# RWKV state as a full 128x128 block, and its diagonal blocks loaded by three transfers instead of one

## The chip, the cores and the metric

One core of a Trainium2 chip runs the whole program. The metric is the time of one execution in microseconds of the device. The engines named here are PE (TensorE: PE for the matmuls, PEld for the loads of their weights), DVE (VectorE), ACT (ScalarE), POOL (GpSimd, which also issues most small DMAs) and SP (SyncE, which issues the loads of the big weights).

## The reference, cut to what matters

Two blocks follow each other on 272 tokens (16 meta tokens and 256 real ones) of width 2048. The first block projects its normed input with `w_in` and runs three mixers side by side, HGRN2 (a), mLSTM (b) and RWKV7 (c), whose outputs are gated, projected and added. The second block has two layers with pooling, a state-space mixer and sparse attention. The change touches the RWKV7 mixer alone.

RWKV7 has 16 heads of width 64, and each has a state S of 64x64. In chunk form, with the decays folded into the operands, and with A, B, K, R and V of one head and one chunk of tokens, the kernel computes:

```
L   = strict lower part of  A B^T                  (per head: tokens x tokens)
u   = (I - L)^-1 ( A S + strict(A K^T) V )
y   = R S + incl(R B^T) u + incl(R K^T) V
S'  = decay * ( S + B^T u + K^T V )
```

The meta tokens (16) are the first chunk, with S = 0; two chunks of 128 real tokens follow.

## The kernel before

**Tiling.** All activations lie with features on the 128 partitions and tokens in the free dimension. One RWKV group is four heads on two partition tiles j = 0, 1: in each tile head hh = 0 owns partitions 0 to 63 and hh = 1 owns 64 to 127. There are four groups, and each has a `front_c` (projections and operands) and a `back_c` (the chunks).

**The projections and their order.** `unit` (L302) streams the weights: a chunk `wraw` of 128x1024 is loaded through SP, ACT copies it to `whi`, DVE forms the rest `wlo`, and PE runs 24 matmuls of 256 to 272 columns into a tile `pj`. `whi` and `wlo` have four buffers each. The mixers' `back_*` generators run beside these projections: every `yield` gives the turn to another stream, and the framework's planner (a simulated timeline) then fixes each engine's order of instructions at build time. On the chip each engine works that order off strictly: what stands behind a waiting instruction waits too. The projections' ACT and DVE steps have raised priority. PSUM tiles named `mx` (`pst`, L433) have four buffers, which all the small matmuls share.

**The diagonal blocks.** `base_start` (L654) gathers the 16x16 diagonal blocks of L for both chunks and the meta tokens (12 blocks on each partition) in `Dc`, writes them to a DRAM tile `ld`, and reads them back through POOL's queue with each row spread to 16 partitions, into `LB` of 15 steps x 12 x 16 (L666). `base_solve` (L669) then inverts these blocks by 15 steps of forward substitution; step j reads only `LB[:, j]`, one DVE product (`yt<-LB,yc`) and one DVE sum (`yc<-yc,yt`). Everything later in the `back_c` of that group needs its result. `LB` has one buffer, and each group fills it once.

**The chunks.** `back_c` (L947) makes the state S of 128 partitions x 2 x 64 after the meta tokens (L971 to L978): eight matmuls that each write one head's 64 partitions, then `ts` with the decay. For each of the two chunks it does the following. `inverse` completes the inverse Y from the blocks. The step that I call **ru** (L987 to L995) computes A S + strict(A K^T) V: for each head a matmul on the 64 rows of that head (`mx<-S,AT`), then one on 128 token rows (`mx<-vT,Lk`), 8 in all. L996 to L1002 multiply by Y (`mx<-ru,Y`). `pair` makes the two masked score matrices. The step that I call **py** (L1007 to L1013) computes y: for each head one matmul of 64 rows by 64 columns of weights (`mx<-RT,S`), then two of 128 rows by 64 columns (`mx<-Rb,u` and `mx<-Rk,vT`), 12 in all, every one into the 64 partitions of its head. After the first chunk the step **pz** (L1015 to L1025) brings S forward with eight matmuls of 64 weight columns and 64 moving columns.

A matmul on f32 operands appears in the trace as two MATMUL instructions (passes). A form such as 64*128 says rows x columns of the weights in the array, and the shape behind it is that of the moving operand.

Of the kernel before, what the change touches and what calls it, by code (L numbers as in the profile page):

```python
# [9 lines left out]
F32 = mybir.dt.float32  # L10
# [3 lines left out]
ALU = mybir.AluOpType  # L14
# [3 lines left out]
P = 128  # L18
NM = 16
# [219 lines left out]
class Kernel:  # L239
    def __init__(self, ctx, tc, ins, out, dbg=None, stop=None):  # L240
        self.ctx, self.tc, self.nc = ctx, tc, tc.nc
        self.ins, self.out, self.dbgs, self.stop = ins, out, dbg or {}, stop
        self.V, self.S, self.G, self.PE = tc.nc.vector, tc.nc.scalar, tc.nc.gpsimd, tc.nc.tensor

# [21 lines left out]
    def act(self, out, in_, func=AF.Copy, **kw):  # L266
        return self.S.activation(out, in_, func, **kw)  # L267

# [154 lines left out]
    def reg(self, *shape, rows=P, name="r"):  # L423

        n = math.prod(shape)
        t = self.rf.tile([P, 544], F32, tag="r", name=name, bufs=self.nrf)[:rows, :n]
        if len(shape) == 2:
            t = t.rearrange("p (a b) -> p a b", a=shape[0])
        elif len(shape) == 3:
            t = t.rearrange("p (a b c) -> p a b c", a=shape[0], b=shape[1])  # L430
        return t
# [222 lines left out]
    def base_start(self, Lb):  # L654

        Dc = self.Dc
        for c in range(2):
            t = self.reg(4, 8, 16, name="db")
            blk = self.cst("blk").unsqueeze(1).unsqueeze(3).to_broadcast([P, 4, 8, 16])
            self.tt(t, Lb[c].rearrange("p h (b u) -> p h b u", u=16), blk, ALU.mult, self.G)  # L660
            for w in (4, 2):
                self.tt(t[:, :, :w], t[:, :, :w], t[:, :, w:2 * w], ALU.add, self.G)
            self.tt(Dc[:, 4 * c:4 * c + 4], t[:, :, 0], t[:, :, 1], ALU.add, self.G)
        ld = self.dr.tile([8, 16 * 192], F32, tag="ld", name="ld", bufs=2)
        self.nc.gpsimd.dma_start(ld.rearrange("b (s f) -> (b s) f", s=16), Dc.rearrange("p a b -> p (a b)"))
        self.nc.gpsimd.dma_start(self.LB.rearrange("p s a b -> p (s a b)"),  # L666
                                 ld[:, :15 * 192].unsqueeze(1).to_broadcast([8, 16, 15 * 192]))

    def base_solve(self):  # L669

        y = self.reg(12, 16, name="yc")
        self.G.tensor_copy(y, self.cst("eye16").unsqueeze(1).to_broadcast([P, 12, 16]))
        tmp = [self.early(12, 16, name="yt") for _ in range(2)]
        for j in range(15):
            t = tmp[j % 2][:, :, j + 1:]
            self.mul(t, self.LB[:, j, :, j + 1:], y[:, :, j:j + 1].to_broadcast([P, 12, 15 - j]))
            self.add(y[:, :, j + 1:], y[:, :, j + 1:], t)
            yield 0.3
        return y
# [110 lines left out]
    def start_c(self):  # L790
        p1 = self.p1
        self.hw0 = p1.tile([P, 16], F32, name="hw0")
        self.ts(self.hw0, self.par("w0", 0, 16), 0.5, ALU.mult)
        self.wup = p1.tile([P, 1024], F32, name="wup")
        self.nc.gpsimd.dma_start(self.wup, self.ins["wup"])
        self.yc = [None] * 4
        self.Dc = p1.tile([P, 12, 16], F32, name="Dc")
        self.G.memset(self.Dc, 0.0)
        self.LB = p1.tile([P, 15, 12, 16], F32, name="LB")

    def front_c(self, g):
        p1, reg = self.p1, self.reg
# [144 lines left out]
    def back_c(self, g, ops):  # L947
        gl, AT, BT, KT, RT, Lm, Lb, bk, bkm, bon, vT, vm, z = ops
        p1, reg = self.p1, self.reg
        f0 = 2 * g  # L950
        fl = lambda t: t.rearrange("p a b -> p (a b)")
        sm = lambda *shape, name, rows=P, bufs=1: p1.tile([rows, *shape], F32, tag="s_" + name, name=name, bufs=bufs)
        heads = [(j, hh, slice(64 * hh, 64 * hh + 64)) for hh in range(2) for j in range(2)]

        pu = self.pst()
        pu3 = pu[:NM, :256].rearrange("p (h v) -> p h v", h=4)
        for i, (j, hh, rr) in enumerate(heads):
            self.mm(pu3[:, i], Lm[:, i], vm[:, j, rr])
        ru = reg(4, 64, rows=NM, name="rum")
        self.act(ru, pu3)  # L960
        base = yield from self.base_solve()
        Ym = base[:NM, 8:]
        yield 1.0
        pu = self.pst()
        pu3 = pu[:NM, :256].rearrange("p (h v) -> p h v", h=4)
        for i in range(4):
            self.mm(pu3[:, i], Ym[:, i], ru[:, i])
        um = reg(4, 64, rows=NM, name="um")
        self.act(um, pu3)
        yield 1.0  # L970
        S = sm(2, 64, name="S", bufs=3)  # L971
        pz_ = self.pst()
        pz3 = pz_[:, :P].rearrange("p (j v) -> p j v", j=2)
        for i, (j, hh, rr) in enumerate(heads):
            self.mm(pz3[rr, j], bkm[:, 0, j, rr], um[:, i], start=True, stop=False)
            self.mm(pz3[rr, j], bkm[:, 1, j, rr], vm[:, j, rr], start=False, stop=True)
        for j in range(2):
            self.ts(S[:, j], pz3[:, j], gl[:, j, 0:1], ALU.mult)  # L978
        yield 1.0

        y = reg(2, NR, name="y")
        for c in range(2):
            strict, incl = self.cst("si")[:, :P], self.cst("incl")
            Y = yield from self.inverse(Lb[c], base[:, 4 * c:4 * c + 4])
            Lk = self.pair(KT, AT, c, strict, "Lk")
            yield 1.0
            ru = reg(4, 64, name="ru")  # L987
            for hh in range(2):
                pu = self.pst()
                pu3 = pu[:, :P].rearrange("p (h v) -> p h v", h=2)  # L990
                rr = slice(64 * hh, 64 * hh + 64)
                for j in range(2):
                    self.mm(pu3[:, j], AT[rr, 2 * j + c], S[rr, j], start=True, stop=False)
                    self.mm(pu3[:, j], Lk[:, 2 * hh + j], vT[:, 2 * j + c, rr], start=False, stop=True)
                self.act(ru[:, 2 * hh:2 * hh + 2], pu3)  # L995
            yield 1.0  # L996
            pu = self.pst()
            pu3 = pu[:, :256].rearrange("p (h v) -> p h v", h=4)
            for i in range(4):
                self.mm(pu3[:, i], Y[:, i], ru[:, i])  # L1000
            u = reg(4, 64, name="u")
            self.act(u, pu3)  # L1002
            yield 1.0
            Rb = self.pair(BT, RT, c, incl, "Rb")
            Rk = self.pair(KT, RT, c, incl, "Rk")
            yield 1.0
            py = self.pst()  # L1007
            py3 = py[:, :256].rearrange("p (j t) -> p j t", j=2)
            for i, (j, hh, rr) in enumerate(heads):
                self.mm(py3[rr, j], S[rr, j], RT[rr, 2 * j + c], start=True, stop=False)  # L1010
                self.mm(py3[rr, j], u[:, i], Rb[:, i], start=False, stop=False)
                self.mm(py3[rr, j], vT[:, 2 * j + c, rr], Rk[:, i], start=False, stop=True)
            self.act(y[:, :, P * c:P * c + P], py3)  # L1013
            yield 1.0
            if c == 0:  # L1015
                pz_ = self.pst()
                pz3 = pz_[:, :P].rearrange("p (j v) -> p j v", j=2)
                for i, (j, hh, rr) in enumerate(heads):
                    self.mm(pz3[rr, j], bk[:, 0, j, rr], u[:, i], start=True, stop=False)
                    self.mm(pz3[rr, j], bk[:, 1, j, rr], vT[:, 2 * j, rr], start=False, stop=True)  # L1020
                S2 = sm(2, 64, name="S", bufs=3)
                self.add(S2, pz3, S)
                for j in range(2):
                    self.ts(S2[:, j], S2[:, j], gl[:, j, 1:2], ALU.mult)
                S = S2  # L1025
                yield 1.0

        pm = self.pst()
        self.mm(pm, self.cst("bd64"), fl(y))
        self.stt(y, pm.rearrange("p (j t) -> p j t", j=2), -1.0 / 64, ALU.mult, y, ALU.add)  # L1030
        yield 2.0
        sq = reg(2, NR, name="sq")
        self.act(sq, y, AF.Square)
        pm = self.pst()
        self.mm(pm, self.cst("bd64"), fl(sq))
        self.rstd(fl(sq), pm, 1.0 / 64, self.eps(1))
        yield 2.0
        for j in range(2):
            self.stt(y[:, j], y[:, j], self.par("ln_g", f0 + j), ALU.mult, sq[:, j], ALU.mult)
            self.stt(y[:, j], y[:, j], self.par("ln_b", f0 + j), ALU.add, bon[:, j], ALU.add)  # L1040
        self.stt(y, y, 0.5, ALU.mult, z, ALU.mult)
        self.dbg(f"c_o{g}", y)
        self.yc[g] = y
# [894 lines left out]
```

## Time and profile before

| | |
|---|---|
| median of 3 runs | 2994.66 us (2994.41 to 2998.49) |
| the profiled execution's own time | 2993.82 us |
| its span | 2992.0 us |
| PE busy | 2932.0 us, 98% of the span, 23566 matmul instructions |
| DVE busy | 2001.8 us, 67% |
| ACT busy | 1429.5 us, 48% |
| POOL busy | 162.3 us, 5% |
| loads of `LB` | 4, 1440.0 KB each |

A busy engine is not the same as a bound one: matmuls overlap in their pipeline, so what counts on PE is the distance from the start of one to the start of the next, and which waits end late. The RWKV work lies in the first third of the span: the first `yt<-LB,yc` starts at 100.4 us and the last matmul with S as weights or moving operand at 878.2 us.

### The profile page before, as it was taken

What the parts mean: (1) busy time and instruction counts of PE and PEld (TensorE: products, weight loads), DVE (VectorE), ACT (ScalarE), POOL (GpSimd) and SP (SyncE); (2) the same over time, 40 slices, a digit from 0 to 9 for tenths busy, and PEclk for the clock granted to TensorE, in tenths of its full rate; (3) what the DMA queues carried; (4) which work ended last, traced back from release to release, by engine and by line L of the source; (5) the groups of instructions that cost most, each with busy time, mean ns of one, the idle gap of its engine ahead of it and who ended that gap; (6) DMA issues with size and microseconds to landing.
All of it is one profiled execution on the core that took longest, in us unless ns stands there. A gap on an engine that the chain in (4) does not pass through costs nothing.

```text
span 2992.0 us, 57144 instructions
## 1 busy us (share of the span) xinstructions
PE 2932.0 (98%) x23566; PEld 2813.2 (94%) x23566; DVE 2001.8 (67%) x3512; ACT 1429.5 (48%) x2043; POOL 162.3 (5%) x317
## 2 busy tenths in 40 slices
PE   8899999999999999999999999999989999999997
PEld 8898999988889999999999899999989999999997
DVE  7657757746645555567976778774568777877555
ACT  6445645435444434456444444444555444544453
POOL 1000001001000000001100000000011000000000
PEclk9999999999999999999999999999999999999999
DMA  6533534524435666566555455555545645555553
GB/s 221 148 113 121 148 100 127 148 86 140 136 105 164 186 187 184 185 199 221 175 168 154 133 162 163 162 187 173 174 157 172 186 142 155 178 179 185 173 187 122
DMA packets 134005, 479.37 MB, mean 160 GB/s; under 512 B 17552, under 2 KB 18064, under 8 KB 133232
## 3 DMA queue, kind: packets, MB, share of 16 engines
q1 hardware_dynamic: 122112, 441.80, 47.7%
q0 software_dynamic: 11200, 32.84, 4.0%
q8 instruction: 184, 3.01, 0.4%
q10 hardware_dynamic: 432, 1.09, 0.1%
q14 instruction: 77, 0.63, 0.1%
HBM read 467.35 MB, written 7.02 MB: 159 GB/s over the span
## 4 chain that ended last, share of the span: by engine, by line
PE 72%; issue 1%; DVE 1%; DMA 1%; ACT 0%; POOL 0%; DVEq 0%; ACTq 0%; POOLq 0%
PE pj L291 64%; PE mx L291 6%; PE mx L295 1%; DMA LB<-ld 1%; DVE out L270 0%; DVE h L270 0%; DVE xl L288 0%; DMA ed<-csd 0%; ACT L267 0%; DMA csd<-cs 0%; DVE wlo L270 0%; ACT whi L267 0%; ACT r L267 0%; DVE mix L288 0%; POOL ed L1816 0%
## 5 line engine op out<-in xcount | busy, mean ns | idle before, releaser
L291 PE MATMUL pj<-xh,whi 128*128 128x272 f32 (+2 forms) x6080 | 1752.4, 289 | 17.6 <-ACT xh L267 14.3
L291 PE MATMUL pj<-xh,wlo 128*128 128x272 f32 (+2 forms) x6080 | 1749.8, 288 | 15.3 <-DVE wlo L270 15.3
L291 PE MATMUL pj<-xl,whi 128*128 128x272 f32 (+2 forms) x6080 | 1746.3, 287 | 1.0 <-DVE xl L288 1.0
L267 ACT ACTIVATE whi<-wraw 128x1024 fp32r<-128x1024 f32 x840 | 887.0, 1058 | 1245.3 <-PE pj L291 1053.5
L270 DVE TENSOR_TENSOR wlo<-wraw,whi 128x1024 fp32r<-128x1024 f32 x840 | 1024.4, 1221 | 558.9 <-ACT whi L267 555.9
L291 PEld LDWEIGHTS pj<-xh,whi 128*128 128x128 f32 x6080 | 1145.5, 189 | 35.2 <-ACT xh L267 14.7
L291 PEld LDWEIGHTS pj<-xh,wlo 128*128 128x128 f32 x6080 | 1150.2, 189 | 27.4 <-DVE wlo L270 16.0
L291 PEld LDWEIGHTS pj<-xl,whi 128*128 128x128 f32 x6080 | 1148.3, 189 | 10.1 <-issue 4.8
L291 PE MATMUL pj<-yl,whi 128*128 128x256 f32 x384 | 108.2, 282 | 0.0
L291 PE MATMUL pj<-yh,wlo 128*128 128x256 f32 x384 | 108.0, 281 | 0.0
L291 PE MATMUL pj<-yh,whi 128*128 128x256 f32 x384 | 107.8, 281 | 0.0
L267 ACT ACT_TABLE_LOAD x79 | 101.4, 1283 | 3.1 <-PEq L1927 1.7
L291 PEld LDWEIGHTS pj<-yh,wlo 128*128 128x128 f32 x384 | 72.4, 189 | 0.0
L291 PEld LDWEIGHTS pj<-yh,whi 128*128 128x128 f32 x384 | 72.4, 189 | 0.0
L291 PEld LDWEIGHTS pj<-yl,whi 128*128 128x128 f32 x384 | 72.2, 188 | 0.0
L291 PE MATMUL pj<-ml,whi 128*128 128x256 f32 x256 | 71.9, 281 | 0.0
L291 PE MATMUL pj<-mh,wlo 128*128 128x256 f32 x256 | 71.8, 281 | 0.0
L291 PE MATMUL pj<-mh,whi 128*128 128x256 f32 x256 | 71.7, 281 | 0.0
L288 DVE SCALAR_TENSOR_TENSOR cx<-ct,hcw,cx 128x271 f32<-128x271 f32 (+2 forms) x144 | 64.3, 493 | 0.0
L291 PEld LDWEIGHTS pj<-mh,wlo 128*128 128x128 f32 x256 | 48.3, 189 | 0.0
L291 PEld LDWEIGHTS pj<-ml,whi 128*128 128x128 f32 x256 | 48.2, 188 | 0.0
L291 PEld LDWEIGHTS pj<-mh,whi 128*128 128x128 f32 x256 | 48.2, 188 | 0.0
(494 smaller groups left out, 2625.1 us busy)
## 6 DMA issues: line engine op xcount, KB each, us to landing
wraw<-in_w_dram SPq DMA_DIRECT2D x838, 512.0 KB, 3.5
L<-csd POOLq DMA_DIRECT2D x32, 256.0 KB, 4.9
LB<-ld POOLq DMA_DIRECT2D x4, 1440.0 KB, 18.6
h<-in_xt_dram POOLq DMA_DIRECT2D x8, 272.0 KB, 8.9
h<-hd POOLq DMA_DIRECT2D x8, 272.0 KB, 3.9
hd<-h POOLq DMA_DIRECT2D x8, 272.0 KB, 2.4
res<-in_xt_dram POOLq DMA_DIRECT2D x8, 256.0 KB, 4.4
hd<-acc POOLq DMA_DIRECT2D x8, 256.0 KB, 2.8
```

The source lines that it names most:

```text
L267: return self.S.activation(out, in_, func, **kw)
L270: return (eng or self.V).tensor_tensor(out=out, in0=a, in1=b, op=op)
L288: return self.V.scalar_tensor_tensor(out=out, in0=a, scalar=s, in1=b, op0=op0, op1=op1)
L291: return self.PE.matmul(out, lhsT, rhs, start=start, stop=stop)
L295: return self.PE.transpose(out, in_, self.cst("ident")[:n, :n])
```

## The change

`LB` becomes three tiles of five steps, each loaded by a DMA of its own on the same POOL queue, one behind the other; `base_solve` reads `LB[j // 5][:, j % 5]`.

S becomes 128 partitions x 2 x 128, with the two heads of a partition tile as the two 64x64 blocks on the diagonal of 128x128 and zeros elsewhere: the state matmuls now take all 128 rows and both heads at once, and their result is multiplied by the decay and by the 0/1 mask `bd64` in one `scalar_tensor_tensor` instead of a `tensor_scalar`. `um` and `u` change their layout so that the two heads of a tile j are neighbours. In py one matmul per j writes S R for both heads, and the other eight follow, for j, for the two operands, for the two heads; each j has a PSUM tile and an ACT copy of its own.

```diff
-        self.nc.gpsimd.dma_start(self.LB.rearrange("p s a b -> p (s a b)"),
-                                 ld[:, :15 * 192].unsqueeze(1).to_broadcast([8, 16, 15 * 192]))
+        for i in range(3):
+            self.nc.gpsimd.dma_start(self.LB[i].rearrange("p s a b -> p (s a b)"),
+                                     ld[:, 960 * i:960 * i + 960].unsqueeze(1).to_broadcast([8, 16, 960]))
...
-            self.mul(t, self.LB[:, j, :, j + 1:], y[:, :, j:j + 1].to_broadcast([P, 12, 15 - j]))
+            self.mul(t, self.LB[j // 5][:, j % 5, :, j + 1:], y[:, :, j:j + 1].to_broadcast([P, 12, 15 - j]))
...
-        self.LB = p1.tile([P, 15, 12, 16], F32, name="LB")
+        self.LB = [p1.tile([P, 5, 12, 16], F32, name=f"LB{i}") for i in range(3)]
...
-        S = sm(2, 64, name="S", bufs=3)
+        S = sm(2, P, name="S", bufs=3)
         pz_ = self.pst()
-        pz3 = pz_[:, :P].rearrange("p (j v) -> p j v", j=2)
-        for i, (j, hh, rr) in enumerate(heads):
-            self.mm(pz3[rr, j], bkm[:, 0, j, rr], um[:, i], start=True, stop=False)
-            self.mm(pz3[rr, j], bkm[:, 1, j, rr], vm[:, j, rr], start=False, stop=True)
-        for j in range(2):
-            self.ts(S[:, j], pz3[:, j], gl[:, j, 0:1], ALU.mult)
+        pz3 = pz_[:, :256].rearrange("p (j v) -> p j v", j=2)
+        for j in range(2):
+            self.mm(pz3[:, j], bkm[:, 0, j], um[:, j], start=True, stop=False)
+            self.mm(pz3[:, j], bkm[:, 1, j], vm[:, j], start=False, stop=True)
+        for j in range(2):
+            self.stt(S[:, j], pz3[:, j], gl[:, j, 0:1], ALU.mult, own, ALU.mult)
...
-            for hh in range(2):
+            for j in range(2):
                 pu = self.pst()
-                pu3 = pu[:, :P].rearrange("p (h v) -> p h v", h=2)
-                rr = slice(64 * hh, 64 * hh + 64)
-                for j in range(2):
-                    self.mm(pu3[:, j], AT[rr, 2 * j + c], S[rr, j], start=True, stop=False)
-                    self.mm(pu3[:, j], Lk[:, 2 * hh + j], vT[:, 2 * j + c, rr], start=False, stop=True)
-                self.act(ru[:, 2 * hh:2 * hh + 2], pu3)
+                self.mm(pu[:, :P], AT[:, 2 * j + c], S[:, j], start=True, stop=False)
+                for hh in range(2):
+                    rr = slice(64 * hh, 64 * hh + 64)
+                    self.mm(pu[:, rr], Lk[:, 2 * hh + j], vT[:, 2 * j + c, rr], start=False, stop=hh == 1)
+                self.act(ru[:, 2 * j:2 * j + 2], pu[:, :P].rearrange("p (h v) -> p h v", h=2))
...
-            py = self.pst()
-            py3 = py[:, :256].rearrange("p (j t) -> p j t", j=2)
-            for i, (j, hh, rr) in enumerate(heads):
-                self.mm(py3[rr, j], S[rr, j], RT[rr, 2 * j + c], start=True, stop=False)
-                self.mm(py3[rr, j], u[:, i], Rb[:, i], start=False, stop=False)
-                self.mm(py3[rr, j], vT[:, 2 * j + c, rr], Rk[:, i], start=False, stop=True)
-            self.act(y[:, :, P * c:P * c + P], py3)
+            py = [self.pst() for j in range(2)]
+            for j in range(2):
+                self.mm(py[j][:, :P], S[:, j], RT[:, 2 * j + c], start=True, stop=False)
+            for j in range(2):
+                for x in range(2):
+                    for hh in range(2):
+                        rr = slice(64 * hh, 64 * hh + 64)
+                        l, r_ = ((u[:, j, rr], Rb), (vT[:, 2 * j + c, rr], Rk))[x]
+                        self.mm(py[j][rr, :P], l, r_[:, 2 * hh + j], start=False, stop=x == 1)
+            for j in range(2):
+                self.act(y[:, j, P * c:P * c + P], py[j][:, :P])
...
-                for i, (j, hh, rr) in enumerate(heads):
-                    self.mm(pz3[rr, j], bk[:, 0, j, rr], u[:, i], start=True, stop=False)
-                    self.mm(pz3[rr, j], bk[:, 1, j, rr], vT[:, 2 * j, rr], start=False, stop=True)
-                S2 = sm(2, 64, name="S", bufs=3)
+                for j in range(2):
+                    self.mm(pz3[:, j], bk[:, 0, j], u[:, j], start=True, stop=False)
+                    self.mm(pz3[:, j], bk[:, 1, j], vT[:, 2 * j], start=False, stop=True)
+                S2 = sm(2, P, name="S", bufs=3)
                 self.add(S2, pz3, S)
                 for j in range(2):
-                    self.ts(S2[:, j], S2[:, j], gl[:, j, 1:2], ALU.mult)
+                    self.stt(S2[:, j], S2[:, j], gl[:, j, 1:2], ALU.mult, own, ALU.mult)
```

## Rows read from the trace of the kernel before

**Rows 1.** The page: PE's busy time, and the chain that ended last by engine.
```profile
PE 2932.0 (98%) x23566; PEld 2813.2 (94%) x23566; DVE 2001.8 (67%) x3512; ACT 1429.5 (48%) x2043; POOL 162.3 (5%) x317
...
PE 72%; issue 1%; DVE 1%; DMA 1%; ACT 0%; POOL 0%; DVEq 0%; ACTq 0%; POOLq 0%
```

**Rows 2.** Timeline of DVE: start, us, instruction, idle time before it and its end.
```profile
84.51 0.28 DVE L285 TENSOR_SCALAR lp<-lp 4x272 f32<-4x272 f32 x1
100.45 0.35 DVE L270 TENSOR_TENSOR yt<-LB,yc 128x180 f32<-128x180 f32 x1 [15.65 <-DMA LB<-ld]
...
534.80 0.35 DVE L270 TENSOR_TENSOR yt<-LB,yc 128x180 f32<-128x180 f32 x1 [2.40 <-DMA LB<-ld]
...
747.25 0.34 DVE L270 TENSOR_TENSOR yt<-LB,yc 128x180 f32<-128x180 f32 x1 [13.34 <-DMA LB<-ld]
...
754.26 0.27 DVE L270 TENSOR_TENSOR yt<-LB,yc 128x120 f32<-128x120 f32 x1
...
762.04 0.22 DVE L270 TENSOR_TENSOR yt<-LB,yc 128x60 f32<-128x60 f32 x1
```

**Rows 3.** Stretches: busy time (instructions) of PE, PEld, DVE, ACT, POOL; granted clock.
```profile
95.20:104.00 8.80, 0.21 (x3) 0.07 (x1) 3.55 (x5) 2.11 (x2) 0.00 (x0) 0.76 0.25 70
104.00:109.80 5.80, 5.80 (x26) 5.80 (x27) 5.80 (x16) 0.71 (x1) 0.00 (x0) 0.50 0.54 182
...
115.50:118.70 3.20, 0.58 (x6) 0.30 (x5) 3.20 (x10) 1.06 (x1) 0.00 (x0) 1.00 0.52 161
120.30:123.70 3.40, 3.40 (x18) 3.40 (x18) 2.61 (x9) 1.94 (x4) 0.00 (x0) 0.50 0.73 233
744.30:750.40 6.10, 0.19 (x2) 0.00 (x0) 3.05 (x8) 1.68 (x3) 0.00 (x0) 0.83 0.05 18
750.40:755.10 4.70, 4.62 (x21) 4.63 (x22) 4.63 (x14) 1.46 (x3) 0.00 (x0) 0.50 0.51 135
```

**Rows 4.** The DMAs: POOL's issues, landing in the view of `LB`, another transfer's landing.
```profile
81.51 0.63 POOL L666 DMA_DIRECT2D LB<-ld  x1 [3.69 <-DMA ld<-Dc]
...
731.40 0.61 POOL L666 DMA_DIRECT2D LB<-ld  x1 [4.02 <-issue]
...
DMA to landing us min/median/max: 15.4/18.6/19.4
...
L<-csd POOLq DMA_DIRECT2D x32, 256.0 KB, 4.9
```

**Rows 5.** Timeline of PE around a ru step and the product with Y.
```profile
858.55 0.43 PE L291 MATMUL mx<-S,AT 64*128 64x64 f32 x2
...
859.28 0.43 PE L291 MATMUL mx<-S,AT 64*128 64x64 f32 x2
...
864.26 1.00 PE L291 MATMUL mx<-ru,Y 128*128 128x64 f32 x8
865.07 0.36 PE L291 MATMUL pj<-xh,whi 128*128 128x256 f32 x1
```

**Rows 6.** Timeline of PE: one head of a py step; full-size matmuls of 128 moving columns.
```profile
876.17 0.43 PE L291 MATMUL mx<-RT,S 64*64 64x128 f32 x2
876.53 0.43 PE L291 MATMUL mx<-Rb,u 128*64 128x128 f32 x2
...
877.11 0.43 PE L291 MATMUL mx<-RT,S 64*64 64x128 f32 x2
...
295.70 0.39 PE L291 MATMUL mx<-att,vT 128*128 128x128 f32 x2
295.93 0.39 PE L291 MATMUL mx<-qe,S 128*128 128x128 f32 x2
```

**Rows 7.** DVE's instructions on S, by the view of that tile (ns, minimum/median/maximum).
```profile
L288 DVE SCALAR_TENSOR_TENSOR S<-S,dec,mx x8: 337/341/343, 188.5 to 470.9; 128x128 f32<-128x128 f32 x8
```

**Rows 8.** Timeline of PE where two halves of the array are in use.
```profile
811.73 0.32 PE L291 MATMUL mx<-Rb,u 128*64 128x128 f32 x1
811.74 0.33 PE L291 MATMUL mx<-u,bk 128*64 128x64 f32 x2
```

More of the change, by code (lines that the diff above doesn't have):

```diff
@@ L967, in back_c @@
             self.mm(pu3[:, i], Ym[:, i], ru[:, i])
-        um = reg(4, 64, rows=NM, name="um")
-        self.act(um, pu3)
+        um = reg(2, P, rows=NM, name="um")
+        self.act(fl(um).rearrange("p (j h v) -> p h j v", j=2, h=2),
+                 pu3.rearrange("p (h j) v -> p h j v", h=2))
         yield 1.0
-        S = sm(2, 64, name="S", bufs=3)
+        own = self.cst("bd64")
+        S = sm(2, P, name="S", bufs=3)
         pz_ = self.pst()
-        pz3 = pz_[:, :P].rearrange("p (j v) -> p j v", j=2)
-        for i, (j, hh, rr) in enumerate(heads):
-            self.mm(pz3[rr, j], bkm[:, 0, j, rr], um[:, i], start=True, stop=False)
-            self.mm(pz3[rr, j], bkm[:, 1, j, rr], vm[:, j, rr], start=False, stop=True)
+        pz3 = pz_[:, :256].rearrange("p (j v) -> p j v", j=2)
         for j in range(2):
-            self.ts(S[:, j], pz3[:, j], gl[:, j, 0:1], ALU.mult)
+            self.mm(pz3[:, j], bkm[:, 0, j], um[:, j], start=True, stop=False)
+            self.mm(pz3[:, j], bkm[:, 1, j], vm[:, j], start=False, stop=True)
+        for j in range(2):
+            self.stt(S[:, j], pz3[:, j], gl[:, j, 0:1], ALU.mult, own, ALU.mult)
         yield 1.0
@@ L987, in back_c @@
             ru = reg(4, 64, name="ru")
-            for hh in range(2):
+            for j in range(2):
                 pu = self.pst()
-                pu3 = pu[:, :P].rearrange("p (h v) -> p h v", h=2)
-                rr = slice(64 * hh, 64 * hh + 64)
-                for j in range(2):
-                    self.mm(pu3[:, j], AT[rr, 2 * j + c], S[rr, j], start=True, stop=False)
-                    self.mm(pu3[:, j], Lk[:, 2 * hh + j], vT[:, 2 * j + c, rr], start=False, stop=True)
-                self.act(ru[:, 2 * hh:2 * hh + 2], pu3)
+                self.mm(pu[:, :P], AT[:, 2 * j + c], S[:, j], start=True, stop=False)
[3 more added lines that the diff above has]
+                self.act(ru[:, 2 * j:2 * j + 2], pu[:, :P].rearrange("p (h v) -> p h v", h=2))
             yield 1.0
             pu = self.pst()
[L998 to L1002, printed above, removed]
+            for j in range(2):
+                for hh in range(2):
+                    o = P * j + 64 * hh
+                    self.mm(pu[:, o:o + 64], Y[:, 2 * hh + j], ru[:, 2 * j + hh])
+            u = reg(2, P, name="u")
+            self.act(fl(u), pu[:, :256])
             yield 1.0
@@ L1006, in back_c @@
             yield 1.0
-            py = self.pst()
-            py3 = py[:, :256].rearrange("p (j t) -> p j t", j=2)
-            for i, (j, hh, rr) in enumerate(heads):
-                self.mm(py3[rr, j], S[rr, j], RT[rr, 2 * j + c], start=True, stop=False)
-                self.mm(py3[rr, j], u[:, i], Rb[:, i], start=False, stop=False)
-                self.mm(py3[rr, j], vT[:, 2 * j + c, rr], Rk[:, i], start=False, stop=True)
-            self.act(y[:, :, P * c:P * c + P], py3)
+            py = [self.pst() for j in range(2)]
[3 more added lines that the diff above has]
+                for x in range(2):
+                    for hh in range(2):
+                        rr = slice(64 * hh, 64 * hh + 64)
[3 more added lines that the diff above has]
+                self.act(y[:, j, P * c:P * c + P], py[j][:, :P])
             yield 1.0
@@ L1016, in back_c @@
                 pz_ = self.pst()
-                pz3 = pz_[:, :P].rearrange("p (j v) -> p j v", j=2)
-                for i, (j, hh, rr) in enumerate(heads):
-                    self.mm(pz3[rr, j], bk[:, 0, j, rr], u[:, i], start=True, stop=False)
-                    self.mm(pz3[rr, j], bk[:, 1, j, rr], vT[:, 2 * j, rr], start=False, stop=True)
-                S2 = sm(2, 64, name="S", bufs=3)
+                pz3 = pz_[:, :256].rearrange("p (j v) -> p j v", j=2)
+                for j in range(2):
+                    self.mm(pz3[:, j], bk[:, 0, j], u[:, j], start=True, stop=False)
+                    self.mm(pz3[:, j], bk[:, 1, j], vT[:, 2 * j], start=False, stop=True)
+                S2 = sm(2, P, name="S", bufs=3)
                 self.add(S2, pz3, S)
                 for j in range(2):
-                    self.ts(S2[:, j], S2[:, j], gl[:, j, 1:2], ALU.mult)
+                    self.stt(S2[:, j], S2[:, j], gl[:, j, 1:2], ALU.mult, own, ALU.mult)
                 S = S2
```

## Prediction

> **What bounds the kernel now.** I read the page first. PE is busy for 98% of the span and DVE for 67%, and 72% of the chain that ended last is PE's, almost nothing DMA's [rows 1]. So the kernel is bound by the order of PE's matmuls: a change gains what it takes out of that order, start to start, or out of PE's idle time. Then I looked in the stretch of the RWKV work for PE's idle time, by the stretches and by DVE's timeline. There are two large holes, both of one kind. DVE reaches the first `yt<-LB,yc` of a group and stands until the load of `LB` lands: from 84.8 to 100.45 us and from 733.9 to 747.25 us [rows 2]. PE lives on for some 10.4 us with the split weights it has, and then stops, at 95.2 and 744.3 us: 8.6 and 5.9 us without work, and behind each hole PE runs at a granted clock of 0.50 (the lower of its two levels, 1.2 GHz) for a while [rows 3]. At the third load the wait is 2.40 us [rows 2], far less than those 10.4, and no hole follows. Last I read PE's timeline in the RWKV steps. Full-size matmuls (128*128) follow each other in 0.11 us a pass, whether 64 columns move (0.81 us for 8) or 128 (0.23 us for 2) [rows 5, 6]. Where the shape in the array changes from one matmul to the next it is slower: the pair `S,AT` and `vT,Lk` takes 0.73 us, 0.18 a pass [rows 5], and one head of py takes 0.94 us for six passes [rows 6].
>
> **Part one: S over the whole array.** PE.
> ru: before, four pairs of 0.73, so 2.92 us [rows 5]. After, per j one state matmul of 128 moving columns and two `vT,Lk`, in all 6 matmuls or 12 passes, all 128*128, at 0.11: 1.34 us. Gain 1.58 us, eight times (four groups, two chunks): 12.6 us.
> py: before, four heads of 0.94: 3.76 us [rows 6]. After, two state matmuls at 0.23 (0.45 us), one change of shape (the four passes from `Rb,u` to the next head take 0.58 where four plain ones take 0.44, so 0.14 us is what a change costs) and eight matmuls of 128*64. These now alternate between the left and the right half of the array. Where that happens before, a pass of `Rb,u` and one of `u,bk` for the other half start 0.01 us apart [rows 8]. If all of them overlap so, two passes cost one 0.11: 8 x 0.11 = 0.9, py 1.5 us. If none does (16 x 0.11), 2.35 us. The row is of two different PSUM tiles, while here both halves write one, so I take 1.7, near the row. Gain 2.06 us, eight times: 16.5 us; ends 11 and 18.
> The Trainium skill says in "TensorE: Matmul & The Clock Gate", Part 3 (packing small matmuls), that matmuls on different column groups of the array run at once, some 4 ns apart. By it py would be 1.5 us and its gain 18 us; the row's 0.01 us agrees, for two tiles.
> pz and the state after the meta tokens: 16 passes of 64 columns and half the width become 8 of full size, and two narrow passes cost about one full one by the same overlap row. I count nothing; the ends are 1 us either way.
> DVE: the 16 `ts` become products with a mask of 128 columns; such an instruction on S takes 0.34 us [rows 7], 5.5 us in all were all of it new, on an engine with a third of the span free. One ACT copy more per py. Both sit beside PE's projections. The cover would be gone only where DVE stands already, which is part two.
> Sum of part one: 29 us; ends 23 (no overlap, pz worse) and 32.
>
> **Part two: LB by thirds.** POOL issues one load in 0.63 us [rows 4], so the third is issued 1.3 us later than now. A load of 1440 KB lands 15.4 to 19.4 us after its issue, one of 256 KB after 4.9 [rows 4]. A straight line between these gives some 7.5 us for 480 KB. One queue serves its transfers in order, I assume, so that the thirds land about 7.5, 13 and 19 us after the issue; the ends for the first are 4.9 and 19.4 plus nothing gained. At the first hole: issue 81.5, first third at 89; DVE, there from 84.8, stands 4 us instead of 15.65. That is within the 10.4 us for which PE has work, so the hole goes. The sixth step came 7.0 us after the first where DVE had least else to do, the eleventh 14.8 us [rows 2]: after 89 that is 96 and 104, behind 94.5 and 100.5, when the second and the last third land. What is late next is thus no DMA. At the second hole (issue 731.4, first third 739, DVE there at 733.9) it is the same: 5 us.
> What goes with the holes: 8.6 and 5.9 us idle; 26 and 21 matmuls at half clock in 5.8 and 4.7 us [rows 3], which cost half of that, 2.6 and 2.2 us (from the 0.22 us of each against 0.12). Together 19.4 us. At 115.5 to 118.7 us PE waits 2.6 us more for DVE, which is behind, and 3.4 us at 0.50 follow (1.7 us) [rows 3]. DVE would still be 4 us behind here, so I count half of these 4.3. Sum of part two: 21.5 us; ends 0 (nothing lands earlier) and 23.6. The other two loads give nothing, since PE has no hole there.
> **Sum.** 29 and 21.5 make 50.5. The profiled execution took 2993.82 us of its own (span 2992.0), so 2943.3; the median of the runs is 0.84 us above it: **2944 us**.
>
> **The rivals.**
> A, the forecast: both parts, own range 2930 to 2956 (both upper ends, and PE idle or half clock elsewhere that goes too; both a fifth short).
> B, the thirds land together. They share the same DMA engines, and if they are served side by side the first lands no earlier than now. For it: nothing before shows two such loads in one queue. Against: the one queue. Part one alone remains: 2965 us. (The Trainium skill, "DMA: Bandwidth & Descriptors", Two DMAs through the same engine are not ordered, says that within one queue of one DMA engine descriptors start in order, though they overlap; by it B falls away, and no run so far shows it.)
> C, PE's gain is not handed on: what comes after it waits for `wlo` or a PSUM tile, of which py now holds two of the four at once. For it: DVE and ACT have fixed orders and lose nothing. Against: DVE's and DMA's share of the ending chain is 1% each, and DVE has a third free [rows 1]. Part two alone: 2972 us.
> D, slower. The planner counts a third as a short transfer and puts the last five steps early in DVE's order, at all four groups, so DVE stands until the last third, 20.6 us after the issue (19.4 and the 1.3 of the later issue). It decides from the point where DVE reaches step eleven more than 10.4 us before that landing. PE then idles up to 10 us four times with 2.4 us of half clock behind each, 50 us where it loses 19.4 today. With part one at its low end, 23, that is 8 us slower: 3002. For it: at 84.8 and 733.9 us DVE came to the first step far too early. Against: the steps were mixed with other work over 15 us and more.
> E, nothing: another order of the planner takes back what is gained, 2994.
>
> **How the numbers follow.** A 0.70, B 0.13, C 0.08, D 0.05, E 0.04. The range from 2929 to 2970 takes in A, B and a part of C. Faster by over 0.2% (6 us, about the least that a measurement of this kernel tells from no change): A, B, C and a little of E, 0.92; within it, 0.04; slower, 0.04.
>
> **What would show it.** Right: ru of 1.3 to 1.4 us with no shape but 128*128 in it; py of 1.5 to 2.4 us, at the low end if the `Rb,u` of the two halves start together; first `LB` thirds landing 5 to 9 us after the issue, DVE waiting under 6 us for each; no PE idle time above 3 us between 80 and 110 or 740 and 760 us, and no clock of 0.50 after it. Wrong: thirds that land within 2 us of each other (B), new PE waits for `wlo` or `mx` in the RWKV stretch (C), DVE waits for the second or last third of 8 us and more (D).

## The result

The changed kernel takes 2955.95 us (median of 4 runs, 2952.79 to 2957.01), the kernel before, run beside it, 2996.57 us (median of 4, 2994.41 to 3000.59). The ratio is 0.9863, with a 95% interval of 0.9848 to 0.9879. The profiled execution took 2952.79 us of its own (span 2951.0), 41.0 us less than that of before; forecast were 50.5. The time lies in the forecast range, 12 us above the point.

The page of the changed kernel: engines, the chain that ended last, the loads of `LB` (KB each, median us from issue to landing).
```profile
PE 2901.7 (98%) x23438; PEld 2795.7 (95%) x23438; DVE 2003.1 (68%) x3512; ACT 1428.7 (48%) x2051; POOL 165.4 (6%) x325
...
PE 94%; DVE 2%; issue 1%; DMA 1%; ACT 1%; POOL 0%; DVEq 0%; ACTq 0%; POOLq 0%
...
LB<-ld POOLq DMA_DIRECT2D x12, 480.0 KB, 9.5
```
PE bounds the kernel as before [rows 1]. The 5100th projection matmul (`pj`, one behind the RWKV stretch) starts at 938.4 us before and at 896.8 us now, 41.6 us earlier, and up to the end of the span (41.0) that lead changes by less than 1 us: the whole gain lies ahead of it. So I sorted all time between one PE start and the next, up to that matmul, by what PE began:

| us of PE, up to the same matmul | before | after | gained |
|---|---|---|---|
| idle stretches over 0.3 us | 20.2 | 9.3 | 10.9 |
| half clock (all shapes), and projections | 632.3 | 621.5 | 10.8 |
| ru, 8 times | 20.4 | 9.4 | 11.0 |
| py, 8 times | 29.6 | 19.8 | 9.8 |
| pz | 4.0 | 4.0 | 0.0 |
| state after the meta tokens | 3.6 | 4.3 | -0.7 |
| projection to mixer, and all other mixer work | 220.3 | 220.3 | 0.0 |

The first two lines are part two of the prediction, 21.7 us where 21.5 were forecast. The rest is part one, 20.1 us where 29 were forecast.

**The holes.** DVE's timeline of the changed kernel: the first `yt` of the first and of the last group of `LB`.
```profile
87.28 0.34 DVE L270 TENSOR_TENSOR yt<-LB,yc 128x180 f32<-128x180 f32 x1 [2.79 <-DMA LB<-ld]
...
714.98 0.35 DVE L270 TENSOR_TENSOR yt<-LB,yc 128x180 f32<-128x180 f32 x1 [8.50 <-DMA LB<-ld]
```
The waits of 15.65 and 13.34 us [rows 2] are 2.79 and 8.50 now, and the one of 2.40 is gone. Stretches of the changed kernel, columns as in [rows 3]:
```profile
84.30:95.20 10.90, 10.90 (x89) 10.90 (x88) 8.11 (x19) 2.98 (x3) 0.00 (x0) 1.00 1.02 219
95.20:104.00 8.80, 8.80 (x71) 8.59 (x69) 8.78 (x22) 3.84 (x6) 0.10 (x1) 1.00 0.75 234
104.00:110.00 6.00, 4.28 (x25) 4.11 (x25) 5.42 (x16) 3.85 (x6) 0.00 (x0) 0.72 0.55 182
...
704.00:715.00 11.00, 11.00 (x93) 10.74 (x92) 2.08 (x3) 2.51 (x4) 2.74 (x9) 1.00 0.99 185
...
732.50:735.00 2.50, 0.85 (x12) 0.56 (x10) 2.33 (x8) 0.78 (x1) 0.10 (x1) 1.00 0.55 187
```
From 95.2 to 104 us, where PE was busy for 0.21 us before, it is busy throughout. What is left are small waits, by the view of PE's waits in the RWKV stretch (us in all, times, longest):
```profile
PE mx L291 <- DVE BKm L270: 2.1, 2, 1.1
PE mx L291 <- DVE yc L270: 1.6, 1, 1.6
PE mx L295 <- DVE c L285: 1.6, 1, 1.6
PE mx L291 <- DVE Lb L270: 1.4, 2, 0.8
PE mx L291 <- ACT sq L267: 1.4, 2, 0.7
PE pj L291 <- DVE wlo L270: 0.6, 1, 0.6
```
The two large holes of before were waits for `wlo` too, of 14.6 us, and are gone. The waits for `BKm`, `yc` and `wlo` and one of the two for `Lb`, 4.9 us together, stand where PE did not wait before. Behind the wait for `c`, at 106.2 us, stand the only 3.4 us at half clock that are left in this stretch; before they were 27.3 us in four pieces.

**The matmuls.** PE's timeline of the changed kernel, a whole ru step:
```profile
819.45 0.39 PE L291 MATMUL mx<-S,AT 128*128 128x128 f32 x2
819.67 0.56 PE L291 MATMUL mx<-vT,Lk 128*128 128x64 f32 x4
820.06 0.44 PE L291 MATMUL mx<-S,AT 128*128 128x128 f32 x2
820.34 0.56 PE L291 MATMUL mx<-vT,Lk 128*128 128x64 f32 x4
820.71 0.36 PE L291 MATMUL pj<-xh,whi 128*128 128x256 f32 x1
```
Twelve passes of one shape in 1.26 us, a little under the 1.34 forecast. The same view, a py step:
```profile
833.01 0.38 PE L291 MATMUL mx<-RT,S 128*128 128x128 f32 x2
833.32 0.43 PE L291 MATMUL mx<-Rb,u 128*64 128x128 f32 x2
833.69 0.49 PE L291 MATMUL mx<-RT,S 128*128 128x128 f32 x2
834.11 0.65 PE L291 MATMUL mx<-Rb,u 128*64 128x128 f32 x6
834.69 0.39 PE L291 MATMUL pj<-xh,wlo 128*128 128x256 f32 x1
...
835.36 0.65 PE L291 MATMUL mx<-Rk,vT 128*64 128x128 f32 x4
835.94 0.39 PE L291 MATMUL pj<-xh,whi 128*128 128x256 f32 x1
...
836.72 0.65 PE L291 MATMUL mx<-Rk,vT 128*64 128x128 f32 x4
837.30 0.39 PE L291 MATMUL pj<-xh,wlo 128*128 128x256 f32 x1
```
This is not the py that I priced. The planner has torn it into three pieces with projections between them, and the state's full-size matmuls stand between `Rb,u` of half size. Each `Rk,vT` piece has four passes, those of one head of both `j`, so of one half of the array (the built program has left and left, then right and right): 0.58 us with nothing beside them. The three pieces take 1.68 + 0.58 + 0.58 = 2.84 us here, the most of the eight steps. Four steps come in three pieces (2.37 to 2.84 us) and four in two (2.19 to 2.48 us); in all eight the last piece is four passes of the right half alone.

### The profile page after: what moved, and what is told of

Its sections match the earlier page's. It is cut to its first block, busy times and chain, and to the rows that moved or that the text cites. A ratio compares the mean times of both kernels' runs of the same rounds, so it can differ in the third digit from the quotient of the medians.

```text
span 2951.0 us, 56913 instructions
## 1 busy us (share of the span) xinstructions
PE 2901.7 (98%) x23438; PEld 2795.7 (95%) x23438; DVE 2003.1 (68%) x3512; ACT 1428.7 (48%) x2051; POOL 165.4 (6%) x325
## 4 chain that ended last, share of the span: by engine, by line
PE 94%; DVE 2%; issue 1%; DMA 1%; ACT 1%; POOL 0%; DVEq 0%; ACTq 0%; POOLq 0%
PE pj L291 80%; PE mx L291 12%; PE mx L295 2%; DVE wlo L270 1%; DMA LB<-ld 0%; ACT L267 0%; DVE out L270 0%; DVE h L270 0%; DVE xl L288 0%; DMA h<-in_xt_dram 0%; DMA ed<-csd 0%; ACT whi L267 0%; POOL db L270 0%; DVE yt L270 0%; DVE yc L270 0%
```

## The experiments

Each is compared with the kernel before, run on the same chip beside it. "Changed" is the kernel with the whole change, 0.9863. The planner makes a new order of instructions for each kernel, so small waits of PE differ between these kernels beyond what the edit names.

**The parts alone.** The changed kernel with the single load of `LB`:
```diff
-for i in range(3): dma_start(self.LB[i], ld[:, 960*i:960*i+960] ...)
+dma_start(self.LB, ld[:, :15*192] ...)
```


> The state as 128x128, LB by one load as before. Theory (both parts gain, and the gains add up): PE's RWKV matmuls as in the changed kernel (S,AT with vT,Lk about 9.5 us, RT,S with Rb,u and Rk,vT about 20 us), but DVE stands 13 to 16 us for LB at the first and fourth group and PE stops there for 6 to 9 us each: 2996 - 22 = 2974 us. Rival (the thirds carry it all, PE's gain is lost elsewhere): 2990 us or more.

2972.47 us, ratio 0.9923 (0.9911 to 0.9936), 24.4 us gained. The kernel before with the three loads and nothing else of the change:

> LB by three loads, the state as before. Theory: the first third lands 6 to 11 us after its issue, no hole of PE over 3 us at the first and fourth group and no 1.2 GHz behind one, ru and py as before (20.4 and 29.6 us): 2996 - 19 = 2977 us. Rival (only the state matters): 2993 us or more, with holes as before.

2976.62 us, ratio 0.9937 (0.9924 to 0.9951), 20.2 us gained. With the state alone both holes and the half clock behind them stay, by the stretches of that kernel:
```profile
95.00:103.60 8.60, 0.13 (x2) 0.13 (x1) 3.61 (x5) 2.11 (x2) 0.00 (x0) 0.74 0.26 74
103.60:110.00 6.40, 6.40 (x31) 6.40 (x32) 6.40 (x18) 1.06 (x1) 0.00 (x0) 0.55 0.49 165
732.00:739.10 7.10, 0.03 (x2) 0.02 (x1) 2.88 (x7) 0.00 (x0) 0.00 (x0) 0.64 0.24 72
```
With the thirds alone DVE waits for `LB` 8.4 us in all, and no hole of PE is left:
```profile
  DVE yt L270: 8.4, 2
...
DMA to landing us min/median/max: 6.4/9.3/14.6
```
The table's lines for ru and py are 9.4 and 19.8 us in the first, 20.4 and 30.1 in the second. So both parts work alone, and each by its own mechanism. Together they gain 40.6 where the sum is 44.6; the intervals, some 4 us to either side, don't tell that from a plain sum.

**Which third matters.** The changed kernel, its thirds issued last first:
```diff
-for i in range(3):
+for i in (2, 1, 0):
```


> The changed kernel with the three loads issued in the order third, second, first, so that step one needs the load that is issued last. Theory A (it counts that the first third is early): DVE stands until 12 to 15 us after the first issue, PE stops again at the first and fourth group for 1 to 5 us each, and the time goes up by 4 to 12 us against 2956. Theory B (it counts that three smaller loads land sooner in all, 12 to 15 us instead of 15 to 19): within 3 us of 2956, no hole over 1 us.

2964.32 us, 0.9896 (0.9882 to 0.991), 8.4 us over the changed kernel. DVE's timeline and the stretches of this run:
```profile
95.73 0.34 DVE L270 TENSOR_TENSOR yt<-LB,yc 128x180 f32<-128x180 f32 x1 [11.97 <-DMA LB<-ld]
```
```profile
94.30:99.20 4.90, 0.01 (x1) 0.00 (x0) 3.47 (x5) 1.06 (x1) 0.00 (x0) 0.80 0.03 10
99.20:104.20 5.00, 4.99 (x22) 4.99 (x23) 5.00 (x14) 0.00 (x0) 0.00 (x0) 0.51 0.60 180
```
The same bytes in the same three loads: with the third that is needed first at the end, DVE waits 11.97 us instead of 2.79, and a hole with half clock behind it is back. (At the fourth group, where I expected one too, DVE waits 5.7 us and no hole forms.) So the early landing of the third that is needed first is what closes the hole. The thirds don't land strictly one after the other, though: in the changed kernel the second lands 1.9 to 2.6 us behind the first in three groups and 0.3 us behind it in the last, and the third 2.8 to 5.7 us behind the second.

**Why py is worth less.** Theory: the tearing. Rival: the halves of the array don't run at once within one PSUM tile. The state matmul can start before `Rk` is there; put last, it can't be run ahead:
```diff
-for j: mm(py[j], S[:, j], RT, start=True, stop=False)
-for j, x in (0, 1), hh: mm(py[j][rr], (u, vT)[x], (Rb, Rk)[x], ...)
+for j, x in (1, 0), hh: mm(py[j][rr], (u, vT)[x], (Rb, Rk)[x], ...)
+for j: mm(py[j], S[:, j], RT, start=False, stop=True)
```


> The changed kernel with the order of the sums in py turned round: Rk first, then Rb, then the state matmul of 128 columns last. Theory (py fell short of its 1.7 us since its state matmul can start long before Rk's mask is done, so that the planner tears py into two to four pieces with projections between them, each with a change of shape, and since the pieces leave halves without a partner): py comes in one or two pieces and takes 1.6 to 2.0 us instead of 2.5, eight times, and the projections beside it lose less: 4 to 10 us faster than 2956. Rival (the halves can't overlap more than they do): py 2.3 us or more, time within 2 us of 2956.

2952.8 us, 0.9854 (0.9841 to 0.9867): 3 us less, short of what was expected, and within the interval of the changed kernel. PE's timeline of this run, the same py step:
```profile
835.11 0.65 PE L291 MATMUL mx<-Rk,vT 128*64 128x128 f32 x4
...
836.48 0.32 PE L291 MATMUL mx<-Rk,vT 128*64 128x128 f32 x1
836.49 0.32 PE L291 MATMUL mx<-Rb,u 128*64 128x128 f32 x1
836.64 0.27 PE L291 MATMUL mx<-Rk,vT 128*64 128x128 f32 x1
836.64 0.54 PE L291 MATMUL mx<-Rb,u 128*64 128x128 f32 x5
...
837.50 0.71 PE L291 MATMUL mx<-RT,S 128*128 128x128 f32 x4
837.96 0.36 PE L291 MATMUL pj<-xh,whi 128*128 128x256 f32 x1
```
The rival falls: where the two halves meet, their passes start 0.00 to 0.01 us apart, though both write one tile (the built program gives these two matmuls the same one). The four `RT,S` passes take 0.46 us, as priced. All eight steps now come in two pieces, and py takes 16.8 us instead of 19.8 (2.1 each). But one piece of a single half still goes ahead, 0.58 us for four passes of the left half. In the second piece the right half has eight passes and the left four, and all twelve take 1.02 us: a half costs nothing where the other has more to do. Of the 3.0 us that py gains, 2.8 come back as idle time of PE (12.1 us by the table's measure, 9.3 in the changed kernel), 2.0 of them in one wait for `c`. The state also by halves, so that py holds one shape:
```diff
-for x in (1, 0): ... ; mm(py[j], S[:, j], RT, stop=True)
+for x in (1, 0, 2): ... with (S[:, j, rr], RT) third
```


> As the kernel with the state last in py, but the state matmul too by halves of 64 columns (four matmuls of 128*64 in place of two of 128*128 for each py). Theory (the halves overlap in one PSUM tile, and a change of shape costs about 0.1 us on each side): the two shapes' change inside py goes, four more passes run beside others: py 1.6 to 2.1 us each, 2949 to 2954 us. Rival (halves in one PSUM tile take turns): 0.2 to 0.4 us more for each py than with the state last, 2954 to 2957 us.

2953.17 us, 0.9857 (0.9844 to 0.9871), py 16.3 us: not told from the run before it. And py as it was before the change, with only ru and the rest changed:
```diff
+for i, (j, hh, rr): mm(py3[rr, j], S[rr, j, rr], RT[rr], ...); mm(... u[:, j, rr], Rb ...); mm(... vT, Rk ...)
```


> The changed kernel, but py as before: per head 64 rows of S, with two halves of 64 columns in twelve matmuls. Theory (on PE the gain of ru and of py are separate and both reach the end): py goes back from 19.8 to about 29.6 us, the time from 2956 to 2964 to 2968 us. Rival (py's shorter matmuls were eaten by the pieces it is torn into): within 3 us of 2956.

2967.62 us, 0.9907 (0.9892 to 0.9922), 11.7 us over the changed kernel, with 31.8 us for py by the table's measure (12.0 more) and a wait of 2.6 us for `wlo`. Against this py the new one is worth some 12 us, against that of the kernel before 9.8, and not 16.5 against either. The two old ones differ because before, in four of the eight steps, py ran passes beside the half-size ones of pz [rows 8] and took 3.42 to 3.56 us; here pz is of full size, and these steps take 4.05.

**Smaller loads.** Is there something left in the waits of 2.79 and 8.50 us?
```diff
-for i in range(3): ... 960 ...   # five steps each
+for i in range(5): ... 576 ...   # three steps each
```


> The changed kernel with LB as five tiles of three steps and five loads of 288 KB. Theory (what counts is that DVE's wait for the first piece is under 10 us, and that is so with thirds): first piece lands 4.5 to 9 us after its issue, DVE waits 0 to 6 us, time within 3 us of 2956. Rival (each load costs a fixed time, so more of them land later in all): last piece more than 16 us after the first issue, DVE waits again, 2960 us or more.

2948.62 us, 0.9843 (0.9829 to 0.9856), 7.3 us under the changed kernel (the two intervals just overlap); I had expected no difference. The view of `LB` in this run:
```profile
  DVE yt L270: 2.5, 2
...
DMA to landing us min/median/max: 4.4/7.7/14.0
```
DVE's waits fall from 11.3 to 2.5 us, and PE's waits for `yc`, `c` and `wlo` and the half clock behind `c` go: PE idles 5.4 us instead of 9.3. I read it so: a wait too short to make a hole still put DVE behind, and PE met that later, as in the wait for `yc` at 734.5 us in the changed kernel, behind DVE's 8.50 us. What the new order of instructions has of it isn't shown apart. With the state matmul last as well:

> Five loads of three steps together with py's order turned round (state last). Theory (the two are independent): the sum of what each gives against the changed kernel, 2949 to 2954 us. Rival (what one of them gives comes out of the same waits for DVE behind LB at the fourth group): no better than the better one alone, 2953 us or more.

2947.09 us, 0.9838 (0.9825 to 0.9852): the lowest median, 8.9 us below the changed kernel, 1.5 below the run before it, which is no difference that these runs tell. Again py gains 2.9 us and PE's idle time grows by 2.6.

**What made one load slow.** The single load of before lands 15.4 to 19.4 us after its issue [rows 4]; all three thirds of the changed kernel have landed 11.8 to 15.0 us after the first one's issue, the same bytes. The packets in the trace say how: before, at most 10 or 11 of the load's 128 packets are in flight at once; of the thirds' 192, 19 or 20. At the second and third group the counts are steadiest: mostly 8 for the single load; for the thirds mostly 16 while the first and the second move side by side, and 8 again when the third is left. The single load's outer dimension is 8. Here `ld` is written twice over, so that one load has 16 rows:
```diff
+ld = dr.tile([16, 16*192]), each row written to two of them
-ld[:, :15*192].unsqueeze(1).to_broadcast([8, 16, 15*192])
+ld[:, :15*192].unsqueeze(1).to_broadcast([16, 8, 15*192])
```


> The changed kernel's state, and LB by one load of 1440 KB as before, but with each of the 8 rows twice in ld (written by two small DMAs), so that the load's outermost dimension is 16 and not 8. Theory (one load moved slowly because about 8 of its packets are in flight at a time, against 16 to 18 with three loads, as the packet records show, and so it isn't its size): it lands 9 to 13 us after its issue, DVE waits 6 to 10 us at the first and fourth group, holes of PE under 2 us: 2954 to 2963 us. Rival (long rows of 11520 bytes are slow, or a single load is): it lands after 15 us or more, holes of 5 us and more as with the state alone: 2970 us or more.

2957.35 us, 0.9864 (0.9847 to 0.988): one load, and the time of the changed kernel. One stop of PE for `c`, of 3.8 us and with half clock behind it, is over the 2 us that I allowed. The view of `LB`:
```profile
  DVE yt L270: 14.7, 2
...
DMA to landing us min/median/max: 8.9/10.2/12.0
```
At most 18 or 19 packets are in flight now, mostly 16, and the whole load lands sooner than the last of three thirds. So the number of rows was the limit, and not the size or the single load. (That each row in DRAM is now read by half as many partitions was not tried apart; the thirds read the same 8 rows and reached 16 packets all the same.) The Trainium skill has a rule for it, in "DMA: Bandwidth & Descriptors", Why a DMA increments its semaphore by 16 and not by 1: a transfer runs on the largest number of DMA engines up to 16 that divides the outermost dimension (other than 1) of both its sides, so on 8 and on 16 here. The counts of 8 and 16 packets agree with it.

Both at once, five loads of 16 rows and the state last:

> Five loads of three steps, the doubled rows in ld, and the state matmul last in py. Theory (the loads no longer bind once DVE waits under 2 us): within 3 us of five loads with the state last, 2947 us; the extra write of ld delays the first piece by about 1 us. Rival (the loads still bind at the fourth group): first piece under 4 us after its issue and 2942 us or less.

2947.48 us, 0.9833 (0.9818 to 0.9848), the same as with 8 rows. DVE waits 1.7 us in all for the loads: by then they bind nothing that these runs tell.

Why three loads of 8 rows fill what one can't was tried with a small load between the thirds:
```diff
+if i < 2: dma_start(self.spc[i], ld[:, :32])   # 8 rows of 128 B; in the control 16 of 64 B
```


> The changed kernel with a spacer behind the first and behind the second third of LB: a load of 8 rows of 128 B into a tile that nothing reads. Open is why one load with outer dim 8 keeps some 8 to 10 packets in flight and three of them 18. Theory: such a load uses eight of the sixteen DMA engines, and the next such load the other eight. A spacer of 8 rows takes a turn, so all three thirds then stand on the same eight engines: at most about 10 packets in flight, the first third lands 6.7 us after its issue as now, the second and third 11 to 13 and 15 to 18 us after theirs (median of all 11 to 13 instead of 9.5, maximum 16 to 20 instead of 13.7). The Trainium skill states such a turn (DMA: Bandwidth & Descriptors, section Why a DMA increments its semaphore by 16 and not by 1). Rival: any loads that are in flight together fill the sixteen engines; then 16 to 18 packets in flight and landings as in the changed kernel, each at most 1.3 us later. The time itself: 2953 to 2960 us by the rival, 2956 to 2970 by the theory, since DVE then may stand at the sixth or the eleventh step.

> As the run before, but each spacer has 16 rows of 64 B, the same 1 KB. It is the control for the two more issues and their work. By the theory a load of outer size 16 uses all sixteen engines and takes no turn, so the thirds still alternate: 16 to 18 packets in flight, landings of 6.7 us for the first and a median of 9.5 to 10.5, maximum 13 to 15. By the rival the same as with the spacer of 8 rows. If both spacers make the landings late, it is the issues, and neither theory is shown. The time: 2953 to 2960 us by both.

2955.64 us, 0.9859 (0.9844 to 0.9874), and 2952.88 us, 0.9852 (0.9835 to 0.9868). The landings, with the spacer of 8 rows:
```profile
DMA to landing us min/median/max: 6.2/9.2/14.0
```
With the spacer of 16 rows:
```profile
DMA to landing us min/median/max: 6.4/8.4/13.7
```
At most 17 to 20 packets are in flight with 8 rows, 19 to 21 with 16, and at the second and third group both go from 8 (the second third is issued later here) to 16 and back to 8. A turn between two sets of eight engines that every load of 8 rows takes would have brought the thirds to a median of 11 us and more. It falls, at least in this form: a spacer of 1 KB may take no turn. The records don't name the DMA engine of a packet, so what puts the second third beside the first stays open.

## Why the prediction was right, and which terms were not

**ru** was right in its mechanism, and 1.6 us too large: 12.6 forecast, 11.0 measured. The new step takes 1.18 us (forecast 1.34). The old one cost 2.55 and not 2.92, since the row I priced it by [rows 5] is of a step with four pairs in a row; in the other seven the planner has put matmuls of one shape together (2.44 to 2.68 us).

**py is the mis-sized term**: 16.5 forecast, 9.8 measured. The old step was right (3.70 against 3.76). The new one takes 2.47 us and not 1.7, just above the upper end of 2.35. That end was made from the passes of one whole, undisturbed step without overlap. The overlap is there, but the planner's order uses it for a part of the passes only, and each further piece has two changes of shape against projections. Where the halves have partners the price was right: a step with the state last takes 2.07 us, and without the 0.58 of its lone piece 1.49, the 1.5 of full overlap. The step that failed is the sentence "These now alternate between the left and the right half": the code does, the order on PE does not. py at 2.1 with the state last, and 12 us lost with the old py, show the size of it. Why it tears by heads I read from the order alone. The two halves of `Rk` come from two masks on DVE, whose timeline in the changed kernel has them 0.93 us apart:
```profile
832.92 0.42 DVE L270 TENSOR_TENSOR Rk<-mx,c 128x256 f32<-128x256 f32 x1
...
833.85 0.42 DVE L270 TENSOR_TENSOR Rk<-mx,c 128x256 f32<-128x256 f32 x1
```
Both were done at 834.27 us, 1.1 us before the first `Rk,vT` piece started. So on the chip no wait for a mask kept the pieces apart, but the order that the planner had fixed; what its timeline took the masks to cost is not shown.

**pz and the meta step** were right at nothing: 0.0 and -0.7 us.

**Part two** was right in its mechanism and, partly by luck, in its sum: 21.7 against 21.5. Of idle time I had 15.8 us to go (8.6, 5.9 and half of 2.6); 10.9 went. The two holes did close, but the wait for `c` stayed with 1.6 us, and 4.9 us of waits are new; those for `BKm` (2.1 us) and `Lb` come with the state alone as well. Of half clock I had 5.7 us to go (2.6, 2.2 and half of 1.7), and 10.8 went, projections included: PE worked 20.8 us at 0.50 before and 3.5 now, and half of the difference, 8.7 us, is my estimate of the clock's share. That 4.9 us too much and 5.1 too little cancelled is the luck. Some 6.8 us at 0.50 from 837.1 us on, behind no hole of PE, were in the profile before and not in my sum, and are gone. The run with the spacer of 8 rows has such a stretch too, and that with 16 has none:
```profile
801.00:808.00 7.00, 7.00 (x31) 5.37 (x30) 2.61 (x3) 0.85 (x2) 0.81 (x2) 0.53 0.00 2
```
PE is busy in all of it. Half of its 6.8 us, 3.4, is what such a stretch costs, and whether a profile has one I can't trace to the change. Nor does a short stop settle it. The wait of 1.58 us for `c` stands in the changed kernel and in the run with the spacer of 16 rows alike, and the stretches behind it, first of the changed kernel and then of that run, differ:
```profile
105.80:112.00 6.20, 6.05 (x40) 5.98 (x41) 4.40 (x14) 4.03 (x7) 0.00 (x0) 0.72 0.52 169
```
```profile
105.40:112.00 6.60, 6.47 (x56) 6.40 (x57) 5.57 (x16) 5.95 (x9) 0.00 (x0) 1.00 0.48 159
```

**The landings** were right for the first third (7.5 forecast; 6.6 to 6.7 in three groups, 10.8 in the last) and wrong behind it: after the first issue I had 13 and 19 us, and 9 to 11 and 12 to 15 were measured. I let the loads go one after the other at the rate of one; the first two moved side by side, with twice as many packets in flight. DVE's wait of 8.50 us in the last group is over the 6 that I allowed, and made no hole, since PE had projections for it: from 704 to 715 us it is busy throughout. The first third of that group, at 10.8, is over the 9 us named as the sign of being right, as py's 2.47 is over its 2.4.

**The rivals.** B needs thirds that land together: reversing them would then cost nothing, and it cost 8.4 us. Its sign was met in part: the first two landed 0.3 us apart in the last group. But side by side they didn't hold each other up, as B had it: in the three other groups the first lands after 6.6 to 6.7 us, against 15.4 us and more of the single load. That one queue serves the loads in order, which the prediction set against B, was not so for these two. C asks for new waits in place of PE's gain: the 4.9 us above, of which 0.6 are for `wlo`, are its part of the truth, an eighth of the gain. D needs a long wait for the second or the last third: none is in DVE's timeline. E is out by 40 us.

## What to carry to other kernels

When steps are scheduled by a planner, price a new group of matmuls by the order that the planner is likely to give it, not by the order in which the code names them: a half of the array only costs nothing when its partner is issued beside it. A wait shorter than the cover makes no hole, and can still be worth removing if the engine that stands has a queue behind it. Before a transfer is cut up, count its packets in flight: the same gain came from one load with twice the rows.

## What the runs showed of the hardware

- A load with an outer dimension of 8 (1440 KB) had mostly 8 and at most 10 or 11 packets in flight and landed in 15.4 to 19.4 us; with 16, it had mostly 16 and at most 18 or 19 packets, and landed in 8.9 to 12.0 us. Three loads of 8 in a row had 16 while two of them moved (at most 19 or 20), and 8 with the last one alone.
- Matmuls on the left and the right half of the array start 0.00 to 0.01 us apart also when both add into one PSUM tile. Eight passes of one half and four of the other took 1.02 us; four of one half alone took 0.58.
- In the changed kernel a PE stop of 1.6 us, for `c`, is followed by 3.4 us at a granted clock of 0.50, and the two waits for `BKm`, of 1.0 and 1.1 us, by none. The same stop for `c` is followed by none in the run with the spacer of 16 rows, so its length alone doesn't decide it.
